# Two-operand SBUF work moved from POOL to DVE, and masks and gates applied from PSUM, in a two-layer hybrid block on one core

## The chip, the cores and the metric

The kernel runs on one core of a Trainium2 chip. The metric is device time in microseconds (us) of one execution. Engines are named as in the profile: PE is the matmul engine (PEld its weight loads), DVE the vector engine, ACT the scalar engine, POOL the GpSimd engine, SP the engine that only issues DMAs. SBUF is the on-chip memory that all engines read, PSUM the accumulators that PE writes and that POOL does not read in this kernel.

## The reference

Two layers, 1024 latent and 256 context tokens, width 1024, all in float32. Each layer does this (last layer: latent tokens only):

```python
h = rms_norm(x, norm_g) * (1 + scale) + shift           # x: latent or context tokens
z = h @ w_in                                            # 1024 -> 29 blocks of 128 columns
a = hyena_branch(...)       # two long convolutions by FFT, gated: x2*conv(x1*conv(v))
b = rwkv_mixer(...)         # bidirectional delta-rule recurrence, 4 heads of 64
c = window_attention(...)   # +-128 tokens and the context, with a sink logit
d = dense_attention(...)    # normalised q/k, rotary positions
mix = concat(a, b, c, d) * silu(gates)
x = x + gate * (mix @ w_out)
```

The output is the latent stream after a last RMS norm.

## The kernel before

Tokens are worked in tiles of 128. Every large matmul is run at full precision as three products: an operand `x` is split into a rounded high part `h` (ACT, `AF.Copy` into a float32r tile) and a low part `x - h`, and high*high, high*low and low*high are summed in PSUM. The low parts are subtractions of two SBUF tiles: `hlo` of the input (L211), `wl` of each block of `w_in` (L232), `wol` of `w_out` (L1081), `ss` of the decay (L509).

The stages of a layer, in the order of the code: the norm and the filters of the hyena (`norm_in`, `hy_filters`), the projection of the recurrence's columns (`Proj.rw`, `chan`), the attention's columns (`Proj.attn`), the recurrence's parallel part (`Rwkv.phase_a`, ten blocks of 128 tokens, with a 32x32 triangular `solve` after blocks 4, 8 and 10), its sequential part (`phase_b`), the gates and the hyena's columns (`Proj.beside`), the hyena itself (`hyena`, and `ctx_hyena` in layer 0), both attentions (`attention`), the output product (`OutProj`). In the first layer `phase_a` runs at about 440 to 700 us of the profile and the hyena with part of an attention beside it at about 1062 to 1210 us; in the second at 1720 to 2000 us and 2318 to 2466 us.

The code writes each stage for itself. The order on each engine is set at build time by the language's scheduler from buffers, dependencies and its own estimate of durations, so stages overlap and a change of engine at one place reorders all engines. An instruction written `nc.any` is put on ACT or DVE by that scheduler. Each engine then runs its own list in order, and waits on semaphores for the others.

Names that the rest uses:

- `PT` is a `tensor_tensor` on POOL, `TT` one on DVE.
- In `hyena`, `forward` multiplies the spectrum `W` (128 x 8 x 2 x 128) with the filter's `Kf`; DVE did the upper half of the eight slots and POOL the lower half (L1409 to L1412). The butterfly `Dft.eight` sends its odd half to DVE (`G`, L1230 to L1235) and its even half and one difference to POOL (L1222 to L1225, L1245). It runs twice in a forward, and four forwards make a layer's hyena.
- In `phase_a` a product in PSUM (`p_g`) is multiplied with a 0/1 mask into `GG`. Of four such products per block two went to DVE directly (L596); the other two were copied to SBUF by ACT (L594) and masked by POOL (L596). `bs` (L559 to L561) is a sum for the readout; `s` (L537) is a power, on POOL.
- In `solve` POOL took the first two rows of each step, DVE the rest (L646, L647).
- In `attention`, `values` made the output `om` out of PSUM `O` in three steps: ACT copied the reciprocal half (L1027), POOL multiplied it with the gate `gt` (L1028), DVE with the values (L1029).

Of the kernel before, what the change touches and what calls it, by code (L numbers as in the profile page):

```python
# [420 lines left out]
class Rwkv:  # L421
# [22 lines left out]
    def phase_a(w, ep, sp, pp):  # L444
# [178 lines left out]
        def solve(i):  # L623
# [13 lines left out]
            PC = 2  # L637
            tmp2 = sp.tile([128, 31 * PC], F32, tag="tmp2", bufs=1, name="tmp2")
            for j in range(31):
                a, q = 31 - j, j + 1  # L640
                c = min(q, PC)
                for e, m, s, z in ((nc.gpsimd, tmp2, 0, c), (eng, tmp, c, q)):
                    if z > s:
                        n = z - s
                        t = m[:P, 0:a * n].rearrange("p (q a) -> p q a", q=n)
                        e.tensor_tensor(t, Lx[:P, j:j + 1, j + 1:].to_broadcast([P, n, a]), X[:, s:z, j:j + 1].to_broadcast([P, n, a]), op=ALU.mult)  # L646
                        e.tensor_tensor(X[:, s:z, j + 1:], X[:, s:z, j + 1:], t, op=ALU.add)  # L647
# [1013 lines left out]
```

## Time and profile before

| | before |
|---|---|
| median of 3 runs | 2606.55 us (2602.04 to 2608.11) |
| profiled execution, its own time | 2599.59 us |
| span in the profile | 2597.8 us |
| mean granted TensorE clock | 0.913 of full speed |
| busy: PE, DVE, ACT, POOL | 88%, 65%, 43%, 39% of the span |

Busy shares are means over stages with different limits; a busy PE may run at either of its clock levels, and a busy DVE may be an instruction that is held up. So the stages are read one by one below.

### The profile page before, as it was taken

What the parts mean: (1) busy time and instruction counts of PE and PEld (TensorE: products, weight loads), DVE (VectorE), ACT (ScalarE), POOL (GpSimd) and SP (SyncE); (2) the same over time, 40 slices, a digit from 0 to 9 for tenths busy, and PEclk for the clock granted to TensorE, in tenths of its full rate; (3) what the DMA queues carried; (4) which work ended last, traced back from release to release, by engine and by line L of the source; (5) the groups of instructions that cost most, each with busy time, mean ns of one, the idle gap of its engine ahead of it and who ended that gap; (6) DMA issues with size and microseconds to landing.
All of it is one profiled execution on the core that took longest, in us unless ns stands there. A gap on an engine that the chain in (4) does not pass through costs nothing. (4 is left out here: it accounts for less than half of the span.)

```text
span 2597.8 us, 45285 instructions
## 1 busy us (share of the span) xinstructions
PE 2294.4 (88%) x16864; PEld 1873.1 (72%) x16864; DVE 1696.6 (65%) x3669; ACT 1105.8 (43%) x2622; POOL 1012.8 (39%) x1279
## 2 busy tenths in 40 slices
PE   7799999889999898878897997998999979887698
PEld 3688678667788786656686887976777868666466
DVE  6985247698734567797344776677886345779933
ACT  5422224444232576545444221344443347654451
POOL 1631223366622114464322233324676211336542
PEclk9899998779999899889998998987799989998799
DMA  7223773544364746411444124335445475641152
GB/s 261 93 90 112 247 219 116 151 143 147 107 228 141 196 150 159 165 33 70 139 129 133 72 74 152 114 112 147 136 133 161 161 201 171 163 154 49 42 162 98
DMA packets 288696, 359.12 MB, mean 138 GB/s; under 512 B 108007, under 2 KB 229910, under 8 KB 283100
## 3 DMA queue, kind: packets, MB, share of 16 engines
q1 hardware_dynamic: 264008, 271.04, 33.6%
q0 software_dynamic: 11232, 70.78, 7.9%
q10 hardware_dynamic: 13236, 14.40, 2.0%
q8 instruction: 133, 2.18, 0.3%
q14 instruction: 87, 0.71, 0.1%
HBM read 227.31 MB, written 128.84 MB: 137 GB/s over the span
## 5 line engine op out<-in xcount | busy, mean ns | idle before, releaser
L232 POOL TENSOR_TENSOR wl<-wr,wh 128x1024 fp32r<-128x1024 f32 x58 | 145.1, 2507 | 276.2 <-ACT wh L231 198.9
L986 DVE TENSOR_REDUCE st<-S 128x1 f32<-128x512 f32 (+1 forms) x320 | 173.2, 557 | 102.0 <-PE S L982 57.7
L245 PE MATMUL acc<-hhi,wh 128*128 128x512 f32 (+1 forms) x896 | 222.8, 387 | 15.0 <-ACT wh L231 10.0
L981 PE MATMUL S<-kp,qs 128*128 128x256 f32 (+2 forms) x384 | 151.0, 402 | 85.5 <-ACT P L996 64.1
L245 PE MATMUL acc<-hlo,wh 128*128 128x512 f32 (+1 forms) x896 | 215.8, 376 | 2.6 <-DVE hlo L211 2.6
L996 ACT ACTIVATE P<-S,st 128x512 f32<-128x512 f32 (+1 forms) x320 | 184.2, 588 | 79.4 <-DVE st L989 74.2
L245 PE MATMUL acc<-hhi,wl 128*128 128x512 f32 (+1 forms) x896 | 216.0, 376 | 0.0
L245 PEld LDWEIGHTS acc<-hhi,wh 128*128 128x128 f32 x896 | 160.8, 198 | 50.4 <-ACT wh L231 11.9
L1012 PE MATMUL pt<-ident,P 128*128 128x128 f32 x976 | 169.0, 296 | 29.8 <-ACT PT L952 23.3
L245 PEld LDWEIGHTS acc<-hlo,wh 128*128 128x128 f32 x896 | 157.8, 193 | 33.5 <-DVE hlo L211 3.1
L952 ACT COPY PT<-pt 128x512 f32<-128x512 f32 (+2 forms) x298 | 141.0, 497 | 88.0 <-PE pt L1012 86.2
L245 PEld LDWEIGHTS acc<-hhi,wl 128*128 128x128 f32 x896 | 155.1, 191 | 31.7 <-issue 3.2
L1012 PEld LDWEIGHTS pt<-ident,P 128*128 128x128 f32 x976 | 122.1, 150 | 61.6 <-ACT PT L952 30.7
L981 PEld LDWEIGHTS S<-kp,qs 128*128 128x128 f32 x384 | 78.5, 205 | 114.9 <-ACT P L996 78.0
L1022 PE MATMUL O<-PT,V 128*64 128x256 f32 x976 | 132.1, 388 | 3.3 <-ACT PT L952 2.7
L982 PE MATMUL S<-kp,qs 128*128 128x256 f32 (+2 forms) x384 | 126.7, 342 | 3.7 <-DMA kp<-qk_d 3.7
L1022 PEld LDWEIGHTS O<-PT,V 128*64 128x64 f32 x976 | 70.6, 138 | 45.6 <-issue 6.7
L340 ACT ACTIVATE qx<-acc 128x256 f32<-128x256 f32 x76 | 29.2, 385 | 171.6 <-PE acc L335 152.5
L231 ACT ACTIVATE wh<-wr 128x1024 fp32r<-128x1024 f32 x58 | 60.7, 1057 | 94.3 <-PE acc L245 75.0
L589 PEld LDWEIGHTS p_g<-AR,BKT 64*128 64x128 f32 x640 | 77.0, 221 | 30.9 <-issue 6.8
L335 PE MATMUL acc<-wh,hhi 128*128 128x256 f32 x608 | 95.0, 298 | 4.5 <-ACT qx L340 2.5
L335 PE MATMUL acc<-wl,hhi 128*128 128x256 f32 x608 | 92.4, 290 | 6.4 <-POOL wl L232 6.4
(404 smaller groups left out, 5918.7 us busy)
## 6 DMA issues: line engine op xcount, KB each, us to landing
IN<-in_d POOLq DMA_DIRECT2D x18, 2048.0 KB, 9.4
wr<-in_w_in POOLq DMA_DIRECT2D x58, 512.0 KB, 4.6
mw<-in_mod_w SPq DMA_DIRECT2D x48, 512.0 KB
in_d<-BK SPq DMA_DIRECT2D x20, 512.0 KB
in_d<-AL SPq DMA_DIRECT2D x20, 512.0 KB
kp<-qk_d SPq DMA_DIRECT2D x32, 320.0 KB
qk_d<-qo SPq DMA_DIRECT2D x72, 128.0 KB
in_d<-GG SPq DMA_DIRECT2D x18, 512.0 KB
```

What stands on the lines that cost most here:

```text
L231: w.k.nc.scalar.activation(h, r, AF.Copy)
L232: w.k.nc.gpsimd.tensor_tensor(lw, r, h.bitcast(F32), op=ALU.subtract)
L245: nc.tensor.matmul(ps[:, :n], a[:, kc * 128:(kc + 1) * 128], b[:, kc, t0:t0 + n], start=(i == 0 and kc == 0), stop=(i == 2 and kc == 7))
L335: nc.tensor.matmul(ps[:, :256], x_[:, kc, t * 128:(t + 1) * 128], w_[:, kc, :], start=(n == 0 and kc == 0), stop=(n == 2 and kc == 7))
L589: nc.tensor.matmul(pg[:, hp, c], BKT[q, hp, c], AR[q, :, hp, half(c)], start=True, stop=True)
L952: nc.any.tensor_copy(o, i)
L981: nc.tensor.matmul(ps[:, w0:w0 + w], qs[:, hd % 2, hd // 2], kp[kv][0][:, t0:t0 + w], start=True, stop=False)
L982: nc.tensor.matmul(ps[:, w0:w0 + w], qs[:, hd % 2, hd // 2], kp[kv][1][:, t0:t0 + w], start=False, stop=not masks)
L986: TR(ng[:, i:i + 1], ps[:, :w0], axis=AX.X, op=ALU.max, negate=True)
L996: nc.scalar.activation(P[:, :w], ps[:, :w], AF.Exp, bias=gm, accum_out=den[:, i:i + 1])
L1012: nc.tensor.transpose(pt[:, i, :], P[:, i * 128:(i + 1) * 128], k.ident)
L1022: nc.tensor.matmul(O[kv * 64:kv * 64 + 64, 0], V[:, t, kv * 64:kv * 64 + 64], PTs[kv][:, i], start=(i == 0), stop=(i == nt - 1))
```

## The change

Products and differences of two SBUF operands that POOL computed are computed on DVE: the low parts of the input, of the `w_in` blocks in `chan` and of `w_out` (not those of `Proj.attn`, which stay on POOL), `ss` and `bs` in `phase_a`, the first two rows of `solve`, the even half of the butterfly and the lower half of the filter product in `hyena`, which becomes one instruction over all eight slots. The masks of `phase_a` and the gates of `attention` are applied by DVE from PSUM, without the copy by ACT. Two kinds of plain copies in `phase_b` go from POOL to `nc.any`.

```diff
                 nc.scalar.activation(h, x, AF.Copy)
-                (nc.vector if kc % 4 == 2 else nc.gpsimd).tensor_tensor(low[:, kc], x, h.bitcast(F32), op=ALU.subtract)
+                nc.vector.tensor_tensor(low[:, kc], x, h.bitcast(F32), op=ALU.subtract)
...
-    def split(w, r, h, lw):
+    def split(w, r, h, lw, eng):
         w.k.nc.scalar.activation(h, r, AF.Copy)
-        w.k.nc.gpsimd.tensor_tensor(lw, r, h.bitcast(F32), op=ALU.subtract)
+        eng.tensor_tensor(lw, r, h.bitcast(F32), op=ALU.subtract)
...
-        w.split(r, h, lw)
+        w.split(r, h, lw, nc.vector)
...
-            PT(ss[1], sig, ss[0].bitcast(F32), op=ALU.subtract)
+            TT(ss[1], sig, ss[0].bitcast(F32), op=ALU.subtract)
...
-                PT(bs, kd[:, 0, :], kd[:, 1, :], op=ALU.add)
-                PT(bs, bs, r_, op=ALU.mult)
-                PT(bs, bs, rv[:, 2, :], op=ALU.mult)
+                TT(bs, kd[:, 0, :], kd[:, 1, :], op=ALU.add)
+                TT(bs, bs, r_, op=ALU.mult)
+                TT(bs, bs, rv[:, 2, :], op=ALU.mult)
...
-                    e = TT
-                    if par:
-                        nc.scalar.activation(o, s, AF.Copy)
-                        s, e = o, PT
-                    e(o, s, gmask[:, d, :z].unsqueeze(1).to_broadcast([128, 4, z, 64]), op=ALU.mult)
+                    TT(o, s, gmask[:, d, :z].unsqueeze(1).to_broadcast([128, 4, z, 64]), op=ALU.mult)
...
-                    nc.gpsimd.tensor_copy(pv[half(1 - c), c], VS[half(1 - c)].rearrange("p (h v) -> p h v", h=4))
+                    nc.any.tensor_copy(pv[half(1 - c), c], VS[half(1 - c)].rearrange("p (h v) -> p h v", h=4))
...
-        nc.scalar.activation(o, O[:, 1], AF.Copy)
-        nc.gpsimd.tensor_tensor(o, o, gt[:, :, t0:t0 + 128], op=ALU.mult)
+        nc.vector.tensor_tensor(o, O[:, 1], gt[:, :, t0:t0 + 128], op=ALU.mult)
         nc.vector.tensor_tensor(o, o, O[:, 0], op=ALU.mult)
...
-            nc.gpsimd.tensor_tensor(w.wl[:, kc, :], r, w.wh[:, kc, :].bitcast(F32), op=ALU.subtract)
+            nc.vector.tensor_tensor(w.wl[:, kc, :], r, w.wh[:, kc, :].bitcast(F32), op=ALU.subtract)
...
-        for a, z, e in ((h, R, TT), (0, h, PT)):
-            s = slice(a, z)
-            e(t[:, s], W[:, s], Kf[:, s, 1:2, :].to_broadcast([p, z - a, 2, 128]), op=ALU.mult)
-            e(W[:, s], W[:, s], Kf[:, s, 0:1, :].to_broadcast([p, z - a, 2, 128]), op=ALU.mult)
-            e(W[:, s, 0], W[:, s, 0], t[:, s, 1], op=ALU.subtract)
-            e(W[:, s, 1], W[:, s, 1], t[:, s, 0], op=ALU.add)
+        TT(t, W, Kf[:, :, 1:2, :].to_broadcast([p, R, 2, 128]), op=ALU.mult)
+        TT(W, W, Kf[:, :, 0:1, :].to_broadcast([p, R, 2, 128]), op=ALU.mult)
+        TT(W[:, :, 0], W[:, :, 0], t[:, :, 1], op=ALU.subtract)
+        TT(W[:, :, 1], W[:, :, 1], t[:, :, 0], op=ALU.add)
```

The rest of the diff replaces `PT` by `TT` in the same way at L1222 to L1225, L1245, L1323, L1417, L1418, L1429, L1493, L1524 and L1546, folds POOL's part of L646 and L647 into DVE's, and turns one more copy (L727) into `nc.any`. The changed file is 15 lines shorter, so in the rows of the change below the lines of the hyena are 10 to 15 less.

Counted over the whole program, DVE takes over 70 instructions that are 1024 elements wide (42 `wl`, 16 `wol`, 8 `H`, 4 `zc`), 103 that are 512 wide (12 `hlo`, 20 `ss`, 36 `GG`, 16 even differences, 16 sums of `W`, 3 of the context) and 200 that are 256 wide (6 `hlo`, 54 `bs`, 4 `GG`, 36 `om`, 96 of the even halves, 4 of the context). The halves of L1409 to L1412 add no instruction but double 32 of DVE's. ACT loses 40 copies of `GG` and 36 of `om` and gets 42 copies of `PV` and 18 of `ST`; DVE gets the other 38 copies of `PV`. POOL keeps 16 `wl`, the residual additions, the powers, the readout's products and its DMAs.

The first place is the input stage of layer 0. DVE before, where `raw` is the normalised input that is scaled in place (L209) and `hlo` its low part:

```order
L209 TENSOR_SCALAR raw<-raw,gs_71,sh_72 128x256 x8
L209 TENSOR_SCALAR raw<-raw,gs_71,sh_72 128x512 x9
L211 TENSOR_TENSOR hlo<-raw,hhi 128x256
L209 TENSOR_SCALAR raw<-raw,gs_71,sh_72 128x512 x3
L211 TENSOR_TENSOR hlo<-raw,hhi 128x256
L209 TENSOR_SCALAR raw<-raw,gs_71,sh_72 128x512 x4
```

DVE of the change at the same place, with the filter's `H` and two `wl` in between:

```order
L209 TENSOR_SCALAR raw<-raw,gs_71,sh_72 128x256 x8
L209 TENSOR_SCALAR raw<-raw,gs_71,sh_72 128x512 x7
L211 TENSOR_TENSOR hlo<-raw,hhi 128x256 x7
L209 TENSOR_SCALAR raw<-raw,gs_71,sh_72 128x512 x2
L211 TENSOR_TENSOR hlo<-raw,hhi 128x256
L209 TENSOR_SCALAR raw<-raw,gs_71,sh_72 128x512 x7
L1307 RECIPROCAL inv<-pn 128x128
L1311 TENSOR_TENSOR H<-H 128x1024
L232 TENSOR_TENSOR wl<-wr,wh 128x1024 x2
L211 TENSOR_TENSOR hlo<-raw,hhi 128x512 x8
```

What POOL did beside the scalings now stands behind and between them in DVE's own list.

The second place is the first forward of the hyena in layer 1. DVE before, where `st` are the attention's row statistics that run in between:

```order
L1234 TENSOR_TENSOR W<-G 128x2x2x128
L1235 TENSOR_TENSOR W<-G 128x2x256
L1409 TENSOR_TENSOR t<-W,Kf 128x1024
L999 TENSOR_REDUCE st<-st 128x1
L1410 TENSOR_TENSOR W<-W,Kf 128x1024
L1002 RECIPROCAL st<-st 128x1
L1411 TENSOR_TENSOR W<-W,t 128x4x128
L1412 TENSOR_TENSOR W<-W,t 128x4x128
```

DVE of the change, the same forward:

```order
L1210 TENSOR_TENSOR W<-s_22112 128x256
L1211 TENSOR_TENSOR W<-s_22112 128x256
L976 TENSOR_REDUCE st<-S 128x1
L1218 SCALAR_TENSOR_TENSOR G<-s_22114,s_22083 128x512
L1219 SCALAR_TENSOR_TENSOR G<-s_22114,s_22083 128x512
L1212 TENSOR_TENSOR W<-s_22113 128x2x128
L1213 TENSOR_TENSOR W<-s_22113 128x256
L992 RECIPROCAL st<-st 128x1
L976 TENSOR_REDUCE st<-S 128x1
L1222 TENSOR_TENSOR W<-G 128x2x2x128
L1223 TENSOR_TENSOR W<-G 128x2x256
L979 TENSOR_REDUCE st<-st 128x1
```

The even half (L1210 to L1213) has joined DVE's list, and the attention's reductions are still spread between the butterfly's instructions.

## Rows read from the trace of the kernel before

**Rows 1.** Part 1 of the page: busy us, share of the span, instructions.

```profile
PE 2294.4 (88%) x16864; PEld 1873.1 (72%) x16864; DVE 1696.6 (65%) x3669; ACT 1105.8 (43%) x2622; POOL 1012.8 (39%) x1279
```

**Rows 2.** Windows: stretch, length, busy us of PE, PEld, DVE, ACT, POOL, clock, DMA.

```profile
72.00:112.00 40.00, 24.11 (x122) 20.18 (x123) 38.14 (x48) 16.06 (x30) 30.83 (x23) 0.70 0.16 53
440.00:700.00 260.00, 232.91 (x1473) 186.35 (x1473) 208.27 (x393) 109.93 (x222) 144.68 (x238) 0.83 0.46 136
1062.00:1210.00 148.00, 109.23 (x686) 86.50 (x684) 137.59 (x208) 65.03 (x176) 94.83 (x70) 0.84 0.12 40
1720.00:2000.00 280.00, 259.90 (x1489) 203.21 (x1488) 217.37 (x418) 120.22 (x233) 159.94 (x277) 0.81 0.46 136
2318.00:2466.00 148.00, 99.89 (x639) 79.45 (x638) 136.97 (x200) 57.38 (x154) 99.19 (x70) 0.80 0.11 35
```

**Rows 3.** DVE waiting, 1062 to 1210 us: us in total, times, longest.

```profile
DVE st L986 <- PE S L982: 4.4, 6, 2.2
```

**Rows 4.** PE waiting, 1062 to 1300 us.

```profile
PE S L981 <- ACT P L996: 24.8, 9, 5.6
...
PE ops L1121 <- ACT woh L1080: 8.2, 4, 3.5
```

**Rows 5.** Timeline of POOL, 2323 to 2338 us: start us, us.

```profile
2326.60 3.32 POOL L1429 TENSOR_TENSOR zc<-zc 128x1024 f32<-128x1024 f32 x1
2329.88 3.32 POOL L1409 TENSOR_TENSOR t<-W,Kf 128x1024 f32<-128x1024 f32 x1
```

**Rows 6.** Timeline of DVE, the same stretch.

```profile
2326.08 1.64 DVE L1409 TENSOR_TENSOR t<-W,Kf 128x1024 f32<-128x1024 f32 x1
...
2327.75 3.25 DVE L1410 TENSOR_TENSOR W<-W,Kf 128x1024 f32<-128x1024 f32 x1
...
2331.04 2.72 DVE L1411 TENSOR_TENSOR W<-W,t 128x512 f32<-128x512 f32 x1
2333.68 0.68 DVE L1412 TENSOR_TENSOR W<-W,t 128x512 f32<-128x512 f32 x1
```

**Rows 7.** Instructions on tile W: ns shortest/median/longest, first and last start.

```profile
L1409 POOL TENSOR_TENSOR t<-W,Kf x8: 2352/2728/3320, 1075.5 to 2430.7; 128x1024 f32<-128x1024 f32 x8
L1410 DVE TENSOR_TENSOR W<-W,Kf x8: 1199/2171/3261, 1076.6 to 2440.6; 128x1024 f32<-128x1024 f32 x8
L1411 DVE TENSOR_TENSOR W<-W,t x8: 676/692/2716, 1079.9 to 2443.9; 128x512 f32<-128x512 f32 x8
```

**Rows 8.** DVE groups, 1062 to 1210 us: busy us, mean ns.

```profile
L1231 DVE SCALAR_TENSOR_TENSOR G<-s,s 128x512 f32<-128x512 f32 x8 | 12.4, 1555 | 0.0
L1230 DVE SCALAR_TENSOR_TENSOR G<-s,s 128x512 f32<-128x512 f32 x8 | 9.1, 1135 | 0.1
L1234 DVE TENSOR_TENSOR W<-G 128x512 f32<-128x512 f32 x4 | 8.5, 2120 | 0.0
L1410 DVE TENSOR_TENSOR W<-W,Kf 128x1024 f32<-128x1024 f32 x4 | 7.9, 1964 | 0.1
```

**Rows 9.** DVE groups, 72 to 112 us.

```profile
L209 DVE TENSOR_SCALAR raw<-raw,gs,sh 128x512 f32<-128x512 f32 x16 | 15.5, 1030 | 0.0
L209 DVE TENSOR_SCALAR raw<-raw,gs,sh 128x256 f32<-128x256 f32 x8 | 6.4, 864 | 0.0
```

**Rows 10.** Instructions on tile raw, 70 to 115 us: ns shortest/median/longest.

```profile
L209 DVE TENSOR_SCALAR raw<-raw,gs,sh x24: 402/676/2628, 73.8 to 94.5; 128x512 f32<-128x512 f32 x16, 128x256 f32<-128x256 f32 x8
```

**Rows 11.** Instructions on tile GG: ns shortest/median/longest.

```profile
L594 ACT ACTIVATE GG<-p_g x40: 374/590/600, 450.1 to 1947.1; 128x512 f32<-128x512 f32 x36, 128x256 f32<-128x256 f32 x4
L596 POOL TENSOR_TENSOR GG<-GG,gmask x40: 718/1278/1503, 452.5 to 1947.7; 128x512 f32<-128x512 f32 x36, 128x256 f32<-128x256 f32 x4
```

**Rows 12.** PE waiting, 430 to 660 us.

```profile
PE p_ar L572 <- DVE rho L555: 7.5, 3, 2.8
PE p_r L618 <- POOL GG L596: 5.2, 4, 3.1
```

**Rows 13.** One POOL group, 1210 to 1300 us.

```profile
L1081 POOL TENSOR_TENSOR wol<-wor,woh 128x1024 fp32r<-128x1024 f32 x8 | 18.9, 2371 | 15.4 <-ACT woh L1080 15.4
```

More of the change, by code (lines that the diff above doesn't have):

```diff
@@ L636, in solve @@
             tmp = sp.tile([128, 256], F32, tag="tmp", bufs=1, name="tmp")
-            PC = 2
-            tmp2 = sp.tile([128, 31 * PC], F32, tag="tmp2", bufs=1, name="tmp2")
             for j in range(31):
[L640 to L647, printed above, removed]
+                a, n = 31 - j, j + 1
+                t = tmp[:P, 0:a * n].rearrange("p (q a) -> p q a", q=n)
+                TT(t, Lx[:P, j:j + 1, j + 1:].to_broadcast([P, n, a]), X[:, :n, j:j + 1].to_broadcast([P, n, a]), op=ALU.mult)
+                TT(X[:, :n, j + 1:], X[:, :n, j + 1:], t, op=ALU.add)
             XR = sp.tile([128, 32, 32], F32, tag="Ld", bufs=1, name="XR")
@@ L723, in stage_b @@
                 for c in range(2):
-                    nc.gpsimd.tensor_copy(pv[half(1 - c), c], VS[half(1 - c)].rearrange("p (h v) -> p h v", h=4))
+                    nc.any.tensor_copy(pv[half(1 - c), c], VS[half(1 - c)].rearrange("p (h v) -> p h v", h=4))
                 PV.append(pv)
             if need_y:
-                nc.gpsimd.tensor_copy(ST[:, 1792:2048], VV[:, 0, :])
+                nc.any.tensor_copy(ST[:, 1792:2048], VV[:, 0, :])
             cols = lambda x: x.rearrange("p a (h e) -> p h a e", h=4)
@@ L1221, in even @@
         o = out.rearrange("p s j e -> p (s j) e")
-        s.PT(out[:, 0], AB[:, 0], AB[:, 1], op=ALU.add)
-        s.PT(out[:, 1], AB[:, 0], AB[:, 1], op=ALU.subtract)
-        s.PT(o[:, 4:8:3], A1, B1[:, ::-1], op=ALU.add)
-        s.PT(o[:, 5:7], A1[:, ::-1], B1, op=ALU.subtract)
+        s.TT(out[:, 0], AB[:, 0], AB[:, 1], op=ALU.add)
+        s.TT(out[:, 1], AB[:, 0], AB[:, 1], op=ALU.subtract)
+        s.TT(o[:, 4:8:3], A1, B1[:, ::-1], op=ALU.add)
+        s.TT(o[:, 5:7], A1[:, ::-1], B1, op=ALU.subtract)
     def odd(s, out, TU, CD):
@@ L1293, in hy_filters @@
     nc, A = k.nc, k.A
-    TT, PT = nc.vector.tensor_tensor, nc.gpsimd.tensor_tensor
+    TT = nc.vector.tensor_tensor
     R, p = R8, 128
@@ L1362, in hyena @@
     nc, A = k.nc, k.A
-    TT, PT = nc.vector.tensor_tensor, nc.gpsimd.tensor_tensor
+    TT = nc.vector.tensor_tensor
     n, p, R = L, 128, R8
@@ L1416, in forward @@
         TT(D[:, 0:2], W[:, 0:4:2], W[:, 1:4:2], op=ALU.subtract)
-        PT(S[:, 0:2], W[:, 0:4:2], W[:, 1:4:2], op=ALU.add)
-        PT(S[:, 2:4], W[:, 4:6], W[:, 6:8], op=ALU.add)
+        TT(S[:, 0:2], W[:, 0:4:2], W[:, 1:4:2], op=ALU.add)
+        TT(S[:, 2:4], W[:, 4:6], W[:, 6:8], op=ALU.add)
         ft.eight(Z, S, D, True)
@@ L1492, in ctx_filters @@
         TT(sm, H[:, 0], H[:, 1], op=ALU.add)
-        PT(H[:, 1], H[:, 0], H[:, 1], op=ALU.subtract)
+        TT(H[:, 1], H[:, 0], H[:, 1], op=ALU.subtract)
         pm = (sm, H[:, 1])
@@ L1523, in ctx_hyena @@
     gx = load(tile_("gx", [2, C]), k.gt_d[0:256, L:TOK].rearrange("(h p) t -> p h t", p=128))
-    PT(gx, gx, zc[:, 2], op=ALU.mult)
+    TT(gx, gx, zc[:, 2], op=ALU.mult)
     ux = []
@@ L1545, in ctx_hyena @@
             TT(Z[:, m, 0], Z[:, m, 0], t[:, 1], op=ALU.subtract)
-            PT(Z[:, m, 1], Z[:, m, 1], t[:, 0], op=ALU.add)
+            TT(Z[:, m, 1], Z[:, m, 1], t[:, 0], op=ALU.add)
         mj = [(m, j) for m in range(2) for j in range(2)]
```

14 lines of the change are left out of this document (6 added, 8 removed).

## The prediction

> **What bounds the kernel now.** I read the page's busy shares first, then the windows by stage, then who waited for whom, and at the end single instructions. The shares say that PE is busy for 88% of the span and DVE for 65% [rows 1]. The windows say that this mean hides two kinds of stage. In most of the span PE is nearly full and DVE has room. In three stretches it is the other way round: in the input stage of layer 0 DVE is busy for 38.1 of 40 us and PE for 24.1; in the two hyena stretches DVE is busy for 137.6 and 137.0 of 148 us, PE for 109.2 and 99.9, at a granted clock of 0.84 and 0.80 [rows 2]. So time can be had, or lost, mainly where DVE is full. The first recurrent phase stands between: DVE 208.3 and POOL 144.7 of 260 us in layer 0, PE 232.9 at a clock of 0.83.
>
> In the hyena stretch DVE's own longest wait is for PE, 4.4 us in all [rows 3]; it waits for POOL in no row of that view. PE there waits 24.8 us for ACT's exponential of the attention, which waits for the row statistics in DVE's list [rows 4]. DVE is the engine to reckon with.
>
> A busy DVE may be a held-up DVE. From 2326.08 to 2333.76 us DVE finished three instructions and POOL two, all on two SBUF operands [rows 5, 6]. The same instructions at their shortest take 1.20, 1.20 and 0.68 us on DVE and 2.35 us on POOL [rows 7]: 3.1 + 4.7 = 7.8 us, and 7.7 us went by. The two engines ran as if they took turns.
>
> **The prices.** Clean DVE prices are the shortest in [rows 7]: 1.20 us for 1024 columns and 0.68 for 512. The difference gives 0.52 per 512 columns, so 0.42 for 256. An instruction is recorded as starting 0.08 us before the one ahead of it ends (2331.04 + 2.72 against 2333.68 [rows 6]), so in a full list each costs 0.08 less: 1.12, 0.60, 0.34.
>
> **The whole program.** DVE takes over 70 x 1.12 + 103 x 0.60 + 200 x 0.34 = 208 us; the filter product's lower halves add 8 x 6 x 0.52 = 25; 38 copies of `PV` and the solve's two rows add an estimated 15: some 250 us. POOL loses roughly three quarters of its 1013 us [rows 1]. If nothing is freed in return, DVE goes from 1697 to 1950 us. What is freed is the time in which its instructions are held up, which has to be read stage by stage.
>
> **Hyena, per layer.** Added per forward: filter product 3.1 us; two sums of `W` 1.2; eight even halves 2.7; two even differences 1.2; together 8.2, for four forwards 33, with two gate products of 1024 and four of attention's `om` 37 us. Freed: `G` at L1231 took 1.555 us instead of 0.68, eight times, 7.0; L1230 3.6; L1234 5.8; L1410 3.1 [rows 8]: 19.5 us from four groups. The same reckoning over all 26 groups of that view gives about 38. So DVE's need stays at about 137 of 148 us. The bounds are +17 us (only the four groups are freed) and -11 us (DVE fills its idle time of 148 - 137). I take -2 per layer, -4 in all: near zero, since nothing that DVE waited for comes sooner, a little below it because the statistics no longer stand behind instructions of 2 to 3 us.
>
> **Input stage.** The scalings at L209 took 1.030 and 0.864 us [rows 9]; the shortest of 256 columns is 0.40 [rows 10], and 0.26 more for 512 gives 0.66. Freed: 16 x 0.37 + 8 x 0.46 = 9.6 us. Added: 12 `hlo` of 512, 6 of 256, one `H` and two `wl`: 7.2 + 2.0 + 1.1 + 2.2 = 12.5 us. But the first rows that PE needs are the scalings themselves, and in the order of the change 15 of them stand in front of any moved work. Bounds +3 and -10; I take -4.
>
> **Recurrent phase, per layer.** Added per block: `ss` 0.60, three `bs` 1.02, two `GG` 1.20: 2.8 us, for ten blocks 28. What hides it is DVE's idle time, 260 - 208 = 52 us in layer 0 and 280 - 217 = 63 in layer 1 [rows 2]; without that cover it costs 28 per layer. Removed: the detour of every second `GG`, an ACT copy of 0.59 us and a POOL product of 1.28 [rows 11], against 0.68 on DVE. PE waited 5.2 us for this `GG` in layer 0 [rows 12]. With that wait gone, `rho` and `BK` on DVE are late next (7.5 us for `rho`). I take -7 for both layers. Bounds are +28 per layer and -14 in all, twice what I take.
>
> **Output weights.** `wol` leaves POOL at 2.37 us each [rows 13] for 1.12 on DVE, which has idle time just behind the hyena. Each frees an input buffer, and PE waited 8.2 us there for the high half, which needs that buffer [rows 4]. I take -3 per layer, -6. Bounds 0 and -16.
>
> **At nothing:** `wl` (42 x 1.12 = 47 us on DVE, hidden by the third of its time that DVE idles [rows 1]; without it, 47 us), the copies of `PV` on ACT, which loses 76 copies and gets 60, and the shorter path of `om`, whose bank PE gets back earlier by a copy and a product.
>
> **Sum:** -4 - 7 - 4 - 6 = -21 us. The profiled execution took 2599.6 us, span and 1.8 us around it, so it would take 2578.6; it is 7 us under the median of the runs, so the median becomes 2606.5 - 21 = 2585 us.
>
> **The Trainium skill.** "SBUF — State Buffer", section "SBUF: two separate sides", says that VectorE and GpSimd share one pair of ports as an exclusive lock: whichever starts first, a VectorE instruction with two SBUF inputs or a GpSimd one, holds it to its end, and the other is blocked. The 7.7 us against 7.8 above agree with it. By that rule the pair, not DVE, would fill the hyena stretches, which is the second rival. "Perfetto Trace Analysis", section "Optimizing Scalar/DVE Operations", says that a saturated DVE may be worth relieving towards Scalar or even GPSIMD, and that between GPSIMD and DVE it might not help. The first half speaks against this change, which loads the full engine and frees ACT; it is the first rival. The measured windows do not yet decide between the halves.
>
> **Rivals.**
>
> *Slower: DVE's list feeds PE too late in the recurrent phase.* What is freed there lies largely in the solve, which PE doesn't wait for at once, while `GG`, `ss` and `bs` stand in line ahead of the next block's `rho`, `BK` and copies. For it: PE already waits for `rho` and `BK`, and two DVE instructions replace none of the chain ahead of them. Against it: 52 us of idle DVE. If half of the 28 us per layer reaches PE, -7 becomes +28 and the sum is +14: 2620 us; if all, 2648. It decides from 7 us per layer on. Chance 0.23.
>
> *Much faster: turns were what filled the hyena.* Then DVE closes its idle time, -11 per layer instead of -2, and the recurrent phase, where POOL was busy for 145 of 260 us, gains some 6 more per layer. Sum -21 - 18 - 12 = -51: 2556 us. For it: [rows 5, 6]. Against it: DVE's waits there were for PE, and its need is unchanged. Chance 0.18.
>
> *No change:* added and freed time cancel everywhere, and the removed waits are replaced by waits for `rho` and for the attention's statistics: 2606 us. Chance 0.15. That the change doesn't take effect is excluded by the order: every listed instruction is on DVE, and only 38 of 98 copies followed it there.
>
> **Numbers.** My forecast has 0.44, with its own range 2568 to 2601 us. A measurement of this kernel tells a difference of about 0.2% (5 us) from none. Faster by more than that: 0.44 + 0.18 = 0.62; within it 0.15; slower 0.23. The range that should hold the time 8 times in 10 leaves out the fuller half of the second rival below 2545 and the all-of-28 case above 2625: 2545 to 2625.
>
> **What would show it.** Right, step by step: L1231 and L1410's successor at about 0.68 and 2.3 us (twice the columns); DVE busy near 137 us in each hyena stretch, at about the same length; L209 near 0.4 to 0.66 us; no wait of PE for `GG` behind POOL; DVE near 1700 us in all. Wrong: DVE well above 1750 us with PE waiting longer for `rho` and `BK` (first rival), or hyena stretches of 137 us or less with a higher clock (second). The scheduler also orders everything anew, so a wait at a place that the change doesn't touch could outweigh all of these.

## The result, and the profile after

The change makes the kernel faster: 2565.97 us (median of four runs, 2558.76 to 2572.42) against 2604.3 us (2601.25 to 2608.11) of the kernel before in the same session. The ratio is 0.9851, 95% interval 0.9818 to 0.9885, so some 39 us less. The prediction had the sign and the range (2585, 2545 to 2625), and a bit over half of the size. The experiments will show that this closeness is worth little: three parts of the change gain 92 us together, and a part that the prediction put at nothing takes 51 of them back.

First the page's busy times; they answer to [rows 1].

```profile
span 2567.9 us, 44589 instructions
...
PE 2291.0 (89%) x16864; PEld 1869.6 (73%) x16864; DVE 1719.0 (67%) x4111; ACT 1099.0 (43%) x2601; POOL 273.1 (11%) x404
```

POOL has lost 740 of its 1013 us and DVE has gained only 22 us, although it took over some 250 us of instructions by the prediction's count. So about 228 us of DVE's time before were no work. A second reckoning agrees: for each group of like DVE instructions (line, tile, size), take what each instruction took above the fast end of its group (the fifth percentile), and add that up over all groups. That gives 287 us before and 60 after: 1696.6 + 250 - 227 = 1720, and the page says 1719.0. Below, this sum is called the held-up time.

The windows by stage, with the columns of [rows 2]: the input stage, then the recurrent phase and the hyena stretch of layer 0, then the same two of layer 1.

```profile
66.00:106.00 40.00, 29.78 (x144) 24.21 (x143) 39.81 (x76) 20.95 (x41) 2.58 (x8) 0.79 0.24 85
428.00:647.00 219.00, 204.55 (x1340) 162.68 (x1341) 187.78 (x422) 96.78 (x200) 13.01 (x13) 0.81 0.53 154
1047.00:1190.00 143.00, 107.07 (x731) 87.70 (x730) 132.92 (x264) 69.33 (x183) 0.00 (x0) 0.89 0.20 69
1697.00:1909.00 212.00, 199.00 (x1287) 156.17 (x1289) 183.29 (x414) 96.02 (x196) 13.71 (x14) 0.83 0.52 153
2284.00:2437.00 153.00, 114.22 (x716) 90.62 (x715) 132.57 (x260) 66.38 (x174) 0.00 (x0) 0.84 0.16 60
```

POOL does nothing in the hyena stretches now. Between the same marks (first to last product of a stage on PE), the recurrent phases went from 237 and 236 us to 219 and 212, and the hyena stretches from 154 and 156 to 143 and 153. The stage from the end of the recurrent phase to the hyena grew, from 382 to 400 us in layer 0 and from 349 to 374 in layer 1: something was given back there.

In the timeline of DVE in a hyena stretch (columns as in [rows 6]) the instructions now have one length each.

```profile
2304.36 1.22 DVE L1414 TENSOR_TENSOR zc<-zc 128x1024 f32<-128x1024 f32 x1
...
2308.64 0.68 DVE L1218 SCALAR_TENSOR_TENSOR G<-s,s 128x512 f32<-128x512 f32 x1
2309.24 0.68 DVE L1219 SCALAR_TENSOR_TENSOR G<-s,s 128x512 f32<-128x512 f32 x1
...
2312.22 2.29 DVE L1394 TENSOR_TENSOR t<-W,Kf 128x2048 f32<-128x2048 f32 x1
...
2315.11 2.28 DVE L1395 TENSOR_TENSOR W<-W,Kf 128x2048 f32<-128x2048 f32 x1
```

The product of `W` over 2048 columns takes 2.28 us, where half of it took 1.964 on average [rows 8]. The mean of the other groups that [rows 8] lists, 1047 to 1190 us:

```profile
L1219 DVE SCALAR_TENSOR_TENSOR G<-s,s 128x512 f32<-128x512 f32 x8 | 5.5, 688 | 0.0
L1218 DVE SCALAR_TENSOR_TENSOR G<-s,s 128x512 f32<-128x512 f32 x8 | 5.5, 688 | 0.0
...
L1223 DVE TENSOR_TENSOR W<-G 128x512 f32<-128x512 f32 x4 | 2.8, 692 | 0.0
```

That is 1555 to 688, 1135 to 688 and 2120 to 692 ns. The same by tile, for the scalings [rows 9, 10], `GG` [rows 11] and the output weights [rows 13]:

```profile
L209 DVE TENSOR_SCALAR raw<-raw,gs,sh x24: 406/540/544, 75.0 to 87.1; 128x512 f32<-128x512 f32 x16, 128x256 f32<-128x256 f32 x8
...
L592 DVE TENSOR_TENSOR GG<-p_g,gmask x80: 415/684/693, 444.7 to 1903.6; 128x512 f32<-128x512 f32 x72, 128x256 f32<-128x256 f32 x8
...
L1070 DVE TENSOR_TENSOR wol<-wor,woh x16: 1215/1225/1227, 1240.0 to 2473.5; 128x1024 fp32r<-128x1024 f32 x16
```

PE's waits in the recurrent phase of layer 0 (420 to 650 us) answer to [rows 12].

```profile
PE p_ar L572 <- DVE rho L555: 4.8, 4, 1.9
...
PE p_r L614 <- DVE GG L592: 0.9, 2, 0.4
```

The wait for `GG` fell from 5.2 to 0.9 us, and the wait for `rho`, which was to be "late next", fell as well, from 7.5 to 4.8.

### The profile page after: what moved, and what is told of

Its sections match the earlier page's. It is cut to its first block, busy times and chain, and to the rows that moved or that the text cites. A ratio compares the mean times of both kernels' runs of the same rounds, so it can differ in the third digit from the quotient of the medians.

```text
span 2567.9 us, 44589 instructions
## 1 busy us (share of the span) xinstructions
PE 2291.0 (89%) x16864; PEld 1869.6 (73%) x16864; DVE 1719.0 (67%) x4111; ACT 1099.0 (43%) x2601; POOL 273.1 (11%) x404
## 4 chain that ended last, share of the span: by engine, by line
PE 45%; DVE 13%; DMA 7%; ACT 5%; issue 1%; SPq 1%; POOL 0%; ACTq 0%; POOLq 0%; DVEq 0%
PE acc L245 12%; PE ops L1110 7%; PE acc L335 4%; PE O L1012 3%; PE pt L1002 2%; DVE st L976 2%; PE S L971 2%; DMA st_d<-ST 2%; DMA kp<-qk_d 1%; PE S L972 1%; DMA qs<-qk_d 1%; PE p_g L589 1%; PE pk L1324 1%; ACT P L986 1%; PE p_w L730 1%
## 5 line engine op out<-in xcount | busy, mean ns | idle before, releaser
L245 PE MATMUL acc<-hhi,wh 128*128 128x512 f32 (+1 forms) x896 | 216.8, 378 | 7.8 <-ACT wh L231 5.5
L231 ACT ACTIVATE wh<-wr 128x1024 fp32r<-128x1024 f32 x58 | 60.7, 1057 | 120.5 <-PE acc L245 112.1
L1112 POOL TENSOR_TENSOR y<-y,xt 128x512 f32<-128x512 f32 x36 | 47.8, 1327 | 542.3 <-DVE y L1111 529.1
L257 ACT COPY zp<-acc 128x512 f32<-128x512 f32 (+1 forms) x66 | 34.6, 532 | 145.6 <-PE acc L245 93.7
```

The costliest lines, as they stand in the source:

```text
L245: nc.tensor.matmul(ps[:, :n], a[:, kc * 128:(kc + 1) * 128], b[:, kc, t0:t0 + n], start=(i == 0 and kc == 0), stop=(i == 2 and kc == 7))
```

## Experiments

**Theory:** POOL and DVE take turns. While POOL runs an instruction that reads SBUF, DVE's instructions on two SBUF operands stand still. POOL needs twice DVE's time, so every product that leaves POOL gives DVE more than it costs. **Rival:** the gain comes only from results that arrive sooner (a slow engine no longer stands in a chain), and DVE pays its added work in full. All times are medians in us; the ratio is to the kernel before in the same session, with its 95% interval; the held-up time is of the profiled execution.

| kernel | us | before | ratio | DVE busy | POOL busy | held up |
|---|---|---|---|---|---|---|
| before | | 2602 to 2608 | | 1696.6 | 1012.8 | 287 |
| the change | 2566.0 | 2604.3 | 0.9851 [0.9818, 0.9885] | 1719.0 | 273.1 | 60 |
| p_hyena | 2586.6 | 2605.4 | 0.9926 [0.9914, 0.9939] | 1671.7 | 761.2 | 183 |
| p_recur | 2591.7 | 2605.4 | 0.9945 [0.9929, 0.996] | 1712.4 | 765.5 | 226 |
| p_split | 2581.7 | 2605.4 | 0.9911 [0.9898, 0.9923] | 1696.7 | 853.7 | 206 |
| p_wl | 2584.0 | 2607.3 | 0.9919 [0.9898, 0.9939] | 1686.7 | 923.6 | 226 |
| p_gatecopy | 2615.1 | 2605.4 | 1.0044 [1.0032, 1.0056] | 1723.2 | 945.0 | 283 |
| a_noboth | 2514.9 | 2607.3 | 0.9653 [0.9627, 0.9679] | 1693.7 | 345.1 | 60 |
| a_nocopy | 2523.4 | 2607.3 | 0.968 [0.9658, 0.9702] | 1709.5 | 315.0 | 59 |
| a_nogate | 2533.6 | 2607.3 | 0.9721 [0.9697, 0.9746] | 1705.1 | 309.8 | 60 |
| n_read | 2592.9 | 2602.4 | 0.9958 [0.9936, 0.9981] | 1761.9 | 494.9 | 130 |
| n_set | 2523.7 | 2602.4 | 0.9698 [0.9674, 0.9723] | 1690.3 | 481.7 | 59 |
| s_st | 2546.2 | 2602.4 | 0.9773 [0.9737, 0.9808] | 1717.8 | 282.6 | 60 |
| s_pv | 2535.6 | 2602.4 | 0.9733 [0.971, 0.9756] | 1705.7 | 308.4 | 55 |
| c_dve | 2534.2 | 2607.6 | 0.9713 [0.9686, 0.974] | 1731.7 | 272.6 | 60 |
| a_y | 2516.2 | 2607.6 | 0.9653 [0.9628, 0.9678] | 1701.8 | 296.7 | 45 |

**One part alone.** Each of these is the kernel before with one part of the change. p_hyena takes the hyena and its filters (`even`, `eight`, the filter product, the gate products):

```diff
-        s.PT(out[:, 0], AB[:, 0], AB[:, 1], op=ALU.add)
+        s.TT(out[:, 0], AB[:, 0], AB[:, 1], op=ALU.add)
...
-        for a, z, e in ((h, R, TT), (0, h, PT)):
+        TT(t, W, Kf[:, :, 1:2, :].to_broadcast([p, R, 2, 128]), op=ALU.mult)
```

> The kernel before with only the hyena's part of the change (butterflies, filter product, sums, filter difference, gate products on DVE). My prediction's term: -4 us. If turns between DVE and POOL filled the hyena stretches: both stretches shorter by about 7 us each, -14 us. If the gain of the whole change (-38) comes from the recurrent phase: 0, and the stretches keep their 154 and 156 us.

Measured 2586.6 us, 19 less. The windows of the two hyena stretches, columns of [rows 2], first of the kernel before:

```profile
1052.00:1206.00 154.00, 116.36 (x744) 93.49 (x743) 139.35 (x214) 71.78 (x194) 95.57 (x71) 0.84 0.17 60
2304.00:2460.00 156.00, 108.86 (x720) 88.75 (x719) 141.92 (x211) 66.23 (x180) 99.62 (x71) 0.81 0.16 60
```

Of p_hyena:

```profile
1060.00:1200.00 140.00, 113.11 (x730) 92.47 (x730) 130.87 (x257) 71.05 (x187) 5.38 (x5) 0.83 0.18 63
2307.00:2448.00 141.00, 107.76 (x725) 89.12 (x724) 131.79 (x257) 69.39 (x186) 3.59 (x5) 0.87 0.18 67
```

DVE is busy for 8 to 10 us less with all of POOL's share added, and idle for some 5 us less. Some 2 to 3 us of the fall are copies and reductions that no longer lie within the shorter stretches. The stretches gained 29 us and the profiled execution only 12: other stages came out longer, the way to the first recurrent phase by 8 us and the recurrent phase of layer 1 by 7.

p_recur takes the recurrent phase (`ss`, `bs`, `GG`, the solve):

```diff
-                    e = TT
-                    if par:
-                        nc.scalar.activation(o, s, AF.Copy)
-                        s, e = o, PT
-                    e(o, s, gmask[:, d, :z].unsqueeze(1).to_broadcast([128, 4, z, 64]), op=ALU.mult)
+                    TT(o, s, gmask[:, d, :z].unsqueeze(1).to_broadcast([128, 4, z, 64]), op=ALU.mult)
```

> The kernel before with only the recurrent phase's part (ss, bs, masks from PSUM, solve on DVE alone). My prediction's term: -7 us. If the removed detour over ACT and POOL carries the gain: -20 us or more, with the phase some 15 to 20 us shorter in each layer and the stages behind it not longer. If what the phase gains is given back behind it, as the two traces read together suggest: 0 to -5.

Measured 2591.7 us, 14 less. The phases came 13 and 17 us shorter; in the profiled execution the stage behind the first took 20 us more, which the profile of one run does not explain. The run moves `ss`, `bs`, the masks and the solve's rows at once; which of them gains is not separated.

p_split takes the lower halves (`hlo`, `wl` of `chan`, `wol`), and p_wl only `wl` of `chan`, which the prediction had put "at nothing":

```diff
-        w.split(r, h, lw)
+        w.split(r, h, lw, nc.vector)
```

> The kernel before with only the low parts moved (hlo, wl of the recurrence's, gates' and hyena's columns, wol). My prediction's terms: -4 for the input stage and -6 for the output weights, -10 us. If the wl on DVE hold up DVE's list in the recurrent phase: 0 to +10. If the input stage does not shorten: -6 or less.

> The kernel before with only the wl of chan moved to DVE. My prediction put this at nothing (hidden by DVE's idle time): 0, and the -24 of all low parts would come from the input stage and the output weights. If a wl that comes late from POOL's list (2.4 us each, behind other POOL work) held up the projection: -10 us or more, in the projection's stages.

Measured 24 us less for all three, 23 for `wl` alone: within the error of the two runs this part is `wl`. Its row on DVE, and the page's busy times of that kernel:

```profile
L232 DVE TENSOR_TENSOR wl<-wr,wh 128x1024 fp32r<-128x1024 f32 x42 | 52.6, 1255 | 40.2 <-ACT wh L231 20.8 <-PE acc L245 17.3 <-issue 1.2
...
PE 2295.7 (89%) x16864; PEld 1870.1 (72%) x16864; DVE 1686.7 (65%) x3716; ACT 1104.7 (43%) x2619; POOL 923.6 (36%) x1237
```

DVE runs these 42 instructions more, 52.6 us, and is busy for 10 us less than before [rows 1]. The rival, by which it pays its added work in full, cannot give that. But how 23 us of time come of it is not shown: but for the input stage, DVE is idle for a fifth or more of each stage that holds a `wl`. A `wl` that comes late is not the answer either, since PE's waits of the kernel before have no row for a `wl` of `chan`. The profiled execution of p_wl is the slowest of its six, 2593.6 us, and is only 6 us shorter than that of the kernel before. A rival that no run here excludes is POOL's own list: without 42 `wl` its other results, and the DMAs that it issues, can come sooner.

p_gatecopy takes the attention's gate from PSUM and lets `PV` and `ST` be copied by any engine:

```diff
-                    nc.gpsimd.tensor_copy(pv[half(1 - c), c], ...
+                    nc.any.tensor_copy(pv[half(1 - c), c], ...
...
-        nc.scalar.activation(o, O[:, 1], AF.Copy)
-        nc.gpsimd.tensor_tensor(o, o, gt[:, :, t0:t0 + 128], op=ALU.mult)
+        nc.vector.tensor_tensor(o, O[:, 1], gt[:, :, t0:t0 + 128], op=ALU.mult)
```

> The kernel before with only the attention's gate applied from PSUM and the sequential phase's copies off POOL. My prediction: 0. If the shorter path of om frees PSUM banks in time for PE: -5 to -10 us.

Measured 10 us more. This part frees hardly any held-up time, 287 to 283 us, and the stage ahead of the hyena grew by 19 and 21 us.

**One part left out.** a_noboth is the change without that last part, a_nocopy keeps only the copies on POOL, a_nogate keeps only the gate as it was.

```diff
-                    nc.any.tensor_copy(pv[half(1 - c), c], ...
+                    nc.gpsimd.tensor_copy(pv[half(1 - c), c], ...
...
-        nc.vector.tensor_tensor(o, O[:, 1], gt[:, :, t0:t0 + 128], op=ALU.mult)
+        nc.scalar.activation(o, O[:, 1], AF.Copy)
+        nc.gpsimd.tensor_tensor(o, o, gt[:, :, t0:t0 + 128], op=ALU.mult)
```

> The change without its attention gate and without the sequential phase's copies (both as before). If the parts add up: -19 - 14 - 24 = -57 us against before. If they overlap (a stretch that one part shortens is not there for the next, or what the gate and copies cost alone is no cost beside the others): about the whole change's -38.

> The change with only the sequential phase's copies PV and ST left on POOL. If these copies, which stand in ACT's and DVE's lists between steps that PE waits for, made the +10 of the gate and copies alone: -48 us against before. If the gate made it: -38, as the whole change.

> The change with only the attention's gate left as before (copy by ACT, product by POOL). If the gate's two products in DVE's list hold the PSUM bank longer than the detour did and made the +10: -48 us against before. If the copies made it: -38.

Measured 92, 84 and 74 us less than before. All three beat both kernels. The three good parts together (92) give more than their sum alone (19 + 14 + 24 = 57), although the held-up time that they free just adds up (104 + 61 + 81 = 246 alone, 227 together). On top of them the gate alone costs 8 us and the copies alone 19, but the two together 51.

Part of the gain is PE's own. The page of a_noboth:

```profile
PE 2268.8 (90%) x16864; PEld 1861.9 (74%) x16864; DVE 1693.7 (67%) x4032; ACT 1090.8 (43%) x2582; POOL 345.1 (14%) x538
```

Of the 75 us between its span and that of the kernel before, 49 are idle time of PE. The other 26 are PE's busy time for the same 16864 products [rows 1], at a mean granted clock of 0.926 instead of 0.913. Over the runs the median clock was about 0.916 before, 0.925 in the change and 0.9315 in a_noboth. No run separates the clock from the waits that went.

**Turns, measured by themselves.** In both kernels POOL does work in every forward transform of a_noboth whose result nobody reads: n_read adds `u` to itself, n_set writes zeros for nearly as long.

```diff
         W = tile_([R, 2, 128], "W", 2, p)
+        dz = tile_([R, 128], "dz", 1, p)
+        for _ in range(8):
+            nc.gpsimd.tensor_tensor(dz, u, u, op=ALU.add)
```

(In n_set: `for _ in range(18): nc.gpsimd.memset(dz, 0.0)`.)

> This is the change without the gate from PSUM and without the moved copies (2514.9 us, ratio 0.965, hyena stretches 139 and 140 us), and in each of the four forward transforms POOL now adds u to itself eight times (128x1024, some 2.35 us each, 19 us per forward, 38 per stretch) into a tile that nobody reads. Theory (turns: while POOL reads SBUF, DVE's instructions on two SBUF operands stand still, and the other way round): hyena stretches of 150 to 170 us, DVE's held-up time up by 25 to 70 us in all from 60, DVE busy above 1715 us; 2540 to 2580 us, ratio 0.975 to 0.990. Rival (what the change gained in the hyena is only that PE and DVE no longer wait for a result of a slow engine; nobody waits for these sums): 2510 to 2522 us, stretches of 139 and 140 us, L1219 at 0.70 us as without them.

> The same kernel, with eighteen memsets of the same unread tile on POOL in the place of the eight sums (128x1024, some 0.95 us each, 17 us per forward): POOL is as busy as with the sums, but reads no SBUF. Theory (turns are for instructions of POOL that read two operands): no or little change, 2510 to 2525 us, stretches of 139 to 143 us. If any busy POOL holds DVE up, it comes out as with the sums, 2540 to 2580 us. Rival of both (POOL's load does not matter): 2510 to 2522 us here and with the sums.

Measured 78 us more than a_noboth for the sums, beyond the theory's upper end, and 9 more for the zeros. The windows of the hyena stretches of a_noboth, columns as above:

```profile
1037.00:1177.00 140.00, 113.96 (x736) 92.92 (x734) 131.17 (x259) 70.82 (x186) 5.40 (x5) 0.83 0.19 66
2247.00:2386.00 139.00, 107.24 (x725) 88.64 (x724) 132.14 (x258) 68.38 (x182) 3.65 (x5) 0.86 0.18 67
```

Of n_read:

```profile
1023.00:1200.00 177.00, 119.57 (x731) 95.67 (x730) 167.87 (x257) 70.34 (x184) 75.81 (x37) 0.78 0.15 50
2269.00:2443.00 174.00, 114.40 (x731) 93.67 (x731) 166.56 (x258) 69.41 (x184) 81.48 (x37) 0.79 0.15 55
```

Of n_set:

```profile
1025.00:1167.00 142.00, 109.30 (x732) 89.65 (x732) 130.98 (x259) 71.52 (x189) 63.51 (x66) 0.87 0.18 62
2242.00:2382.00 140.00, 104.68 (x729) 85.68 (x728) 131.46 (x258) 69.65 (x186) 63.53 (x68) 0.90 0.18 67
```

The sums themselves, by tile in n_read, and then their busy time on POOL in the two stretches:

```profile
L1392 POOL TENSOR_TENSOR dz<-u x64: 1888/2218/4152, 1026.1 to 2396.1; 128x1024 f32<-128x1024 f32 x64
...
1023.00:1200.00 177.00, 71.82 (x32) 0.78 0.15 50
2269.00:2443.00 174.00, 76.96 (x32) 0.79 0.15 55
```

DVE ran about as many instructions in all three (257 to 259). Each stretch holds four forwards and so 32 sums, twice what the expectation reckoned with: 71.8 and 77.0 us of POOL. DVE's busy time rose by 36.7 and 34.4 us, and the stretches by 37 and 35. So a microsecond of these sums cost DVE about half a microsecond, and what DVE lost the stretch lost in full. The two stretches make 72 of the 78 us; the runs of n_read scatter from 2579 to 2608 us, and the profiled one, 2581 us, is among the shortest. With 58 and 60 us more of POOL writing zeros, DVE's time did not move (131.0 and 131.5). The timeline of n_read shows which DVE instructions stand still; first POOL, then DVE over the same microseconds.

```profile
1052.64 1.19 POOL L1018 TENSOR_TENSOR om<-om,gt 128x256 f32<-128x256 f32 x1 [7.88 <-ACT om L1017]
1053.80 18.35 POOL L1392 TENSOR_TENSOR dz<-u 128x1024 f32<-128x1024 f32 x7
```

```profile
1050.96 2.29 DVE L1398 TENSOR_TENSOR t<-W,Kf 128x2048 f32<-128x2048 f32 x1
1053.17 1.61 DVE L976 TENSOR_REDUCE st<-S 128x1 f32<-128x512 f32 x3
1054.70 3.13 DVE L1399 TENSOR_TENSOR W<-W,Kf 128x2048 f32<-128x2048 f32 x1
...
1058.15 2.52 DVE L1400 TENSOR_TENSOR W<-W,t 128x1024 f32<-128x1024 f32 x1
1060.59 2.91 DVE L1401 TENSOR_TENSOR W<-W,t 128x1024 f32<-128x1024 f32 x1
```

Just ahead of the sums the product of 2048 columns takes 2.29 us; beside them, one of 1024 takes 2.5 and 2.9 instead of 1.22. The reductions, which read one operand in PSUM, keep their pace of half a microsecond each.

The mechanism of the theory stands: POOL's work on two SBUF operands is paid by a DVE whose list is full, although nobody waits for these sums. So the rival falls for the stretches that DVE fills.

The price is lower than the theory has it. At the place of [rows 5, 6] the two engines took turns in full, 7.7 us for 3.1 of DVE's products and 4.7 of POOL's at their shortest. Over a whole stretch of n_read 32 sums at their shortest, 1.89 us, are 60 us, and DVE lost 36.7 and 34.4, so a part of the sums ran beside it. A sum thus cost DVE 1.1 us, about what DVE needs for such a product itself, 1.22 us. So it is not shown that every product that leaves POOL gives DVE more than it costs. Over the kernel the two about cancel: DVE is busy for 1696.6 us before, 1719.0 in the change and 1693.7 in a_noboth. Beside the turns, results that come sooner can carry a part of the gain, and no run separates them: DVE's idle time in the hyena and PE's wait for `GG` fell as well.

**What the copies cost.** The first idea was ACT's list: a copy into `ST` waits there for the DMA that empties `ST`, and the attention's exponentials wait behind it. s_st puts only the copies into `ST` back on POOL, s_pv only those into `PV`, c_dve puts all of them on DVE.

```diff
-                nc.any.tensor_copy(ST[:, 1792:2048], VV[:, 0, :])
+                nc.gpsimd.tensor_copy(ST[:, 1792:2048], VV[:, 0, :])
```

> The whole change, but the 18 copies into ST stay on POOL; the 80 copies into PV are on ACT and DVE as in the change. Theory (a copy into ST waits for the DMA that empties ST, and what stands behind it in ACT's list, the attention's exponentials and copies, waits too): nearly all that the copies cost comes back, 2515 to 2540 us, ratio 0.965 to 0.974; ACT waits for no DMA of ST. Rival (the PV copies' load on ACT and DVE, some 0.4 and 0.3 us each, 28 us in all): 2555 to 2575 us, as the change.

> The whole change, but the 80 copies into PV stay on POOL; the 18 copies into ST are on ACT as in the change. Theory (the copies into ST cost it): 2555 to 2575 us, as the change, with 15 to 25 us of waits of ACT for the DMA of ST. Rival (the PV copies' load, or their waits for the DMA into IN, cost it): 2515 to 2540 us. If both come back nearly whole, the order as a whole and not one copy decides.

> The whole change with all 98 copies (into PV and ST) on DVE. Theory A (what the copies cost is ACT's list: an ACT copy waits for a DMA and the attention's exponentials stand behind it): most of the 43 us between the change and the copies on POOL comes back, 2520 to 2545 us. Theory B (a copy that waits for a DMA holds up any list that has other work, and DVE's is the fuller one): no better than the change, 2555 to 2600 us, with DVE waiting for the DMAs of IN and ST where ACT did. Theory C (the planned order of the attention's work between, not the waits): anywhere from 2520 to 2570 us, with waits of DVE for these DMAs of under 10 us.

Measured 2546, 2536 and 2534 us: by the ratios 20, 31 and 36 us of the 45 that a_nocopy has over the change come back. The six runs of s_st scatter from 2528 to 2561 us, so its share is the least certain. Neither copy is the one that costs, so the first idea, that `ST` alone does it, falls. Of the waits, all engines, first the change:

```profile
POOL bv L828 <- ACT ST L717: 65.9, 2, 35.8
...
ACT ST L717 <- DMA st_d<-ST: 25.3, 11, 4.4
```

a_nocopy:

```profile
POOL ST L717 <- DMA st_d<-ST: 81.4, 10, 14.7
...
POOL PV L714 <- DMA IN<-in_d: 60.7, 6, 13.3
```

c_dve:

```profile
DVE ST L717 <- DMA st_d<-ST: 17.9, 11, 3.4
```

On POOL these waits are long (81.4 and 60.7 us) and cost little, since nobody waits for POOL there. ACT in the change waits 25.3 us and DVE in c_dve 17.9, and both have other work queued behind. The time of c_dve lies where its expectation puts it if ACT's list is what costs. Yet c_dve, with a wait on DVE not much shorter, has most of the loss back, and s_pv has 31 us back with ACT still waiting 18.8 us for that DMA, so the wait alone isn't the whole cause. One sign is common to the two slow kernels: POOL's `bv` waits for ACT's copy into `ST` for 65.9 us in two waits, and in p_gatecopy for 64.9, but for 19.4 in s_pv and not at all in a_nogate. It is no cause by itself, for in c_dve `bv` waits 55.1 us for DVE.

What the traces show best is the place. In layer 1 the loop over blocks runs, on PE, from the first to the last of the products `p_y` of L805 (first and last start at the end of the row). The change:

```profile
L805 PE MATMUL p_y<-S,ST x144: 218/218/268, 2027.5 to 2202.6; 64*64 64x64 f32 x144
```

a_nocopy:

```profile
L805 PE MATMUL p_y<-S,ST x144: 218/218/268, 2003.5 to 2155.9; 64*64 64x64 f32 x144
```

That is 175 against 152 us. By the same row it is 173 in p_gatecopy, and 152 to 159 in the kernel before and in all the other variants. Only the two kernels that have the gate and leave both copies to the scheduler are slow there. In this loop of the change PE was busy for 154.2 of 176 us, in a_nocopy for 139.2 of 153, and it ran 82 pairs of `S` products of the attention instead of 73. It is 82 in p_gatecopy too, and 73 in every other kernel. So 15 of the 23 us are PE's busy time with attention that the planned order puts into the loop, and 8 are idle time. The loop is not all of the loss: against a_noboth the profiled execution of the change is 45 us longer, 25 between the recurrent phase and the hyena of layer 1, where the loop lies, 12 at the same place of layer 0 and 13 in the hyena stretch of layer 1; the other stages came out 6 us shorter. Why the two edits together do that, these runs don't settle.

**The last product on POOL.** a_y is a_noboth with the residual's addition into `y` on DVE too.

```diff
-                nc.gpsimd.tensor_tensor(y[:, s], y[:, s], xt[:, s], op=ALU.add)
+                nc.vector.tensor_tensor(y[:, s], y[:, s], xt[:, s], op=ALU.add)
```

> The change without the gate from PSUM and without the moved copies (2514.9 us), with the residual's addition into y (36 of 128x512, 1.30 us each on POOL) on DVE as well, the costliest product of two SBUF operands left on POOL. Theory (turns): ml at L1103 falls from 1862 to about 1225 ns, which frees 11 us of DVE in the output stages for 36 x 0.60 = 22 us of additions; these stages keep PE about full, so the time stays within 8 us: 2507 to 2523 us. Rival (the taking of turns costs here as much as in the hyena): 2495 to 2507 us.

Measured 2516.2 us, ratio 0.9653 as without it. The instructions on tile `ml` of a_noboth, then of a_y:

```profile
L1103 DVE TENSOR_TENSOR ml<-mx,mh x18: 1224/2052/2056, 1235.5 to 2490.7; 128x1024 fp32r<-128x1024 f32 x18
```

```profile
L1103 DVE TENSOR_TENSOR ml<-mx,mh x18: 1215/1218/1226, 1229.0 to 2486.2; 128x1024 fp32r<-128x1024 f32 x18
```

The turn is gone (2052 to 1218 ns in the middle) and the time stays: in the output stages DVE has room and PE is the bound, so a held-up DVE costs nothing there.

## Why the prediction was right in sign and wrong in size

**The terms of the sum were mis-sized, and two entries "at nothing" were not nothing.** Each entry against what it measured alone:

| entry | forecast | measured |
|---|---|---|
| hyena | -4 | -19 (p_hyena) |
| recurrent phase, both layers | -7 | -14 (p_recur) |
| `wl` of `chan` | 0 | -23 (p_wl) |
| input stage and `wol` | -10 | about -1 (p_split less p_wl) |
| copies of `PV` and `ST`, path of `om` | 0 | +10 alone, +51 on top of the rest |

**Hyena.** The step was "DVE's need stays at about 137 of 148 us", with 37 us added and 38 freed, and a value "near zero, since nothing that DVE waited for comes sooner". The two sides were sized nearly right: like by like, the instructions that DVE had before took 41 and 43 us less in p_hyena, and those that it got took some 37 by the prediction's way of counting. The rest of the fall of the need, to 131 us, is mainly the 2 to 3 us of copies and reductions that lie outside the shorter stretch. The value is what failed: DVE's idle time, which was to stay, fell from 15 and 14 us to 9, and the stretches came out 14 and 15 us shorter, beyond the bound of -11. The argument took DVE's waits for PE as given; that they are PE's waits for DVE's statistics, seen from the other side, is a reading that no run tested by itself. In the change as a whole the second stretch kept 153 us, with DVE busy for only 132.6. PE's waits there (2284 to 2437 us), first in the change, then in a_nocopy (2238 to 2378 us, a stretch of 140):

```profile
PE S L971 <- ACT P L986: 35.0, 9, 7.2
```

```profile
PE S L971 <- ACT P L986: 20.4, 7, 5.2
```

So the change as a whole shows less than this part can do.

**Recurrent phase.** The step that PE's wait for `GG` goes had the mechanism and half of the size. `GG` hardly stands in PE's way in the change, but `rho`, which was to be late next, came sooner: over the kernel PE waits for it 10.7 us instead of 11.8. The value of -7 was half of its bound, and the bound was met. In the change the phases are 18 and 24 us shorter. The phase of layer 1 before, to be held against the row of 1697 to 1909 us above:

```profile
1719.00:1955.00 236.00, 215.90 (x1297) 167.22 (x1297) 184.28 (x353) 107.84 (x220) 125.82 (x196) 0.78 0.47 140
```

Of its 24 us 17 are PE's busy time, 215.9 to 199.0 us for about as many products, at a granted clock of 0.83 instead of 0.78. The prediction has no term for that.

**`wl` at nothing.** The step was "47 us on DVE, hidden by the third of its time that DVE idles". It asked who hides the added work, and not what POOL's 42 times 2.4 us did to DVE. By the held-up time they held DVE up by some 60 us (287 to 226), more than the 53 us that were added, so DVE paid nothing for them. By which path 23 us of time came of it stays open. This is the largest error of the sum on the gaining side, and the prediction had the row for it: the turns of [rows 5, 6] were weighed for the hyena, in the second rival for the recurrent phase, and not for `wl`.

**Input stage and output weights.** -4 and -6 were forecast; what p_split has over p_wl is about -1, with an error of some 6 us. The prices were about right: in the change 540 and 406 ns for the scalings against the estimate of 660 and 400, 1.225 us for `wol`; PE's wait for `woh` fell there from 8.2 [rows 4] to 4.5 us. But the stages that hold them came out within 3 us of before in p_split (267, 197 and 126 us against 270, 200 and 126).

**Copies and `om` at nothing.** This step failed on the losing side. The work was counted (ACT loses 76 copies and gets 60), but not what a copy that waits for a DMA does in a list with other work behind it, and nothing was said of the order around it. The runs show the loss and where it lies: half of it in the loop over blocks of layer 1, the rest mainly at the same place of layer 0 and in the hyena of layer 1. They leave open why it needs both edits.

**The sum** was -21 and the change measured -39, because a gain of 92 that was put at 21 and a loss of 51 that was put at 0 offset each other. That the measured time lies within the range is luck. DVE's total was forecast right, "near 1700 us", for a reason that the prediction didn't follow to its end: if DVE takes 250 us and stays at 1700, the turns had cost it 250 us.

**The rivals.** "Much faster: turns were what filled the hyena", 2556 us with a chance of 0.18, has the mechanism that n_read shows, and a_noboth went 41 us past it. Its sign was stretches of 137 of the 148 us, 11 less, with a higher clock: in the change layer 0 met it (154 to 143 us, 0.84 to 0.89), layer 1 did not (156 to 153 us, 0.81 to 0.84). "Slower: DVE's list feeds PE too late" fell: the wait for `rho` got no longer. The Trainium skill's "SBUF — State Buffer", section "SBUF: two separate sides", says that a DVE instruction with two SBUF inputs and a GpSimd one lock each other out; n_read agrees with it in kind (71.8 and 77.0 us of sums per stretch, 36.7 and 34.4 us more of DVE), and the reverse, POOL held up, is in the 3.32 us of [rows 5]. The Trainium skill's "Perfetto Trace Analysis", section "Optimizing Scalar/DVE Operations", would relieve a saturated DVE towards other engines, and says that between GpSimd and DVE this might not help. The runs go further: DVE, full in the hyena, got 8 to 10 us emptier by taking POOL's products over.

## What to carry to other kernels

Before an elementwise product is put on POOL or taken from it, compare a DVE instruction's mean with the shortest of its kind: the difference, added up over the kernel, is an estimate of what POOL takes from DVE, and it is paid where DVE is the bound, even when nobody waits for POOL's result. Hold it against what DVE needs for the products itself: here the two were about equal. Move copies that wait for a DMA apart from the products: here they cost 19 us alone, and 51 together with another edit that cost 8. When a change bundles edits, run it without each of them: here the best version is a part of the change, 2515 us, and the whole hides it.

## What the runs showed of the hardware

- POOL's sums of two SBUF operands took about half their time from DVE (71.8 and 77.0 us of sums per stretch, 36.7 and 34.4 us more of DVE's busy time), while 58 and 60 us of POOL's memsets took none (131.2 to 131.0 and 132.1 to 131.5 us).
- DVE's scalings at L209, with one SBUF tensor in and one out and a scalar per partition, were held up too: 1030 and 864 ns on average beside a working POOL [rows 9], 540 and 406 ns in the change. Reductions of a PSUM operand were not: three took 1.61 us beside POOL's instructions in n_read.
